# A one-core decoder block on Trainium2: DRAM writes of turned tiles on ScalarE's queue, residual additions three steps on, double units shifted by one, an FFN's initial chunks spread out

## The chip, the core and the metric

The kernel runs on one core of one Trainium2 chip. The core has a matrix engine (TensorE: PE for its matmuls and PEld for its weight loads in the profile), VectorE (DVE), ScalarE (ACT), GpSimd (POOL) and SyncE (SP). Each engine works through its own list of instructions in order and waits on semaphores where it needs another engine's result. DMAs are issued from SP, ACT or POOL. The metric is the time on the device in microseconds; lower is better.

## What is computed

One decoder block on 256 tokens of width 2048, all in float32. The reference, cut to its frame:

```python
h = x
h = h + 0.5 * swiglu(rms_norm(h, ffn1_norm), ffn1_w_gate, ffn1_w_up, ffn1_w_down)
n = rms_norm(h, mix_norm)
rq, rk, rv, rg, sq, sk, sv = split(n @ w_in)
ret = silu(rg) * group_norm(retention(rope(rq), rope(rk), rv)) * ret_gn_gain
swa = sliding_window_attention(rope(sq), rope(sk), sv, swa_sinks)
h = h + concat(ret, swa) @ w_out
h = h + memory_cross_attention(rms_norm(h, xa_norm), rms_norm(mem, mem_norm), xa_wq, xa_wkv, xa_wo)
h = h + 0.5 * swiglu(rms_norm(h, ffn2_norm), ffn2_w_gate, ffn2_w_up, ffn2_w_down)
out = rms_norm(h, final_norm)

def swiglu(x, w_gate, w_up, w_down):
    return (silu(x @ w_gate) * (x @ w_up)) @ w_down
```

The FFNs are 5632 wide and hold most of the weights. The memory has 256 tokens too.

## The kernel before

**Tiles and precision.** The residual h stands transposed in four tiles (blocks) of 128 partitions by 4 × 256. Weights come from HBM in pieces of 128 × 1024 floats (512 KB), on SP's queue, into eleven landing tiles `wf` (L65, L359). `split` (L368) makes of each piece a rounded part `wh` on ScalarE (L81) and a remainder `wl` on VectorE (L86); there are four tiles of each. A product is three matmuls (`three`, L638): high by high, high by low, low by high, all recorded as L641.

**Steps.** The whole block is one list of steps (`all_steps`, L322), run in order by `run_stream` (L386). A step uses one piece of weights in 12 matmuls of 512 columns. A `Unit` (L164) makes 512 output columns from the blocks of its input and calls `done` with two PSUM banks. Each step first issues the tasks that are due, then the splits of the step `LOOKAHEAD` = 3 places further on and the loads of 4 more; a plain step moves a counter, `clock`, by 1.

**Tasks.** `later(delay, fn)` (L113) puts off a piece of work to the step `delay` on. Its instructions on TensorE, ScalarE and VectorE are tied behind what those engines were given before (`run`, L143); instructions without such a tie can be moved by the compiler's scheduler. Up to step `FIRST` (L35, 15) all engines' orders are pinned as written, and the pieces of those steps are loaded ahead.

**Twins, chunks and double units.** In the FFNs a `Twin` (L185) makes gate and up (or two blocks of a down projection) together. One of the four input blocks is multiplied with seven products in place of eight, on sums and differences of quarters, as in Strassen's method. Such a product is a chunk, named P1 to P7, with 6 matmuls, one split and, for P4 to P7, a difference of two pieces on VectorE (L235); it moves `clock` by 0.5. P1, P5, P6 and P3 begin the four PSUM banks, P1, P5, P6 and P7 are followed by copies and additions (`keep` to `spread`, L260 to L275), and the plain steps of the other blocks add to the banks afterwards. A unit whose index is in `DOUBLE` (L39, used at L717) treats two blocks so and has 8 plain steps; another has 12. Every twin but the first of an FFN is `ahead`: its P1, P5, P6, P3, P7 are strewn among the steps of the unit before it. For the first twin of an FFN, P1 and P5 follow the last two steps of the gate and up of block 0, and P6, P3, P2, P7 come right after those. The sums of an input block, which the chunks multiply with, are made by `sums_of` (L297) in three tasks one step apart: scaling on ScalarE, four sums on VectorE (L290), the split.

**Turning a tile.** A result comes out with tokens on the partitions and is needed with features there. `cross` (L608) does this: two 32 × 32 block transposes on VectorE into `t4k` (L615), one step later a DMA write of 512 KB into a DRAM box (L619), another step later four DMA reads back in the other order (L624), and after `delay` steps a task that uses the tile. `TURN` is 6. There are two `t4k` tiles. Write and reads are issued by GpSimd.

**Residual additions.** `to_h` (L644) takes a projection's output through `cross` and adds it to h (L656) in the task at the end; that task also makes the next norm's scaled block (L81, L525) and its squares (L558, L562). `Norm.finish` (L567) adds the squares on VectorE (L570), sums them over the partitions with small matmuls (L573) and takes the root on GpSimd. The norm's scale is applied after the next projection, so matmuls can begin before the norm is finished.

The order of the work: FFN1 (blocks 0 to 3 of its width and a down projection of them, 4 to 7 and their down projection, 8 to 10 and theirs), the mixer's projections with retention and sliding-window attention between them, w_out, the projections and attention of the memory, xa_wo, FFN2 as FFN1, and the final norm.

Of the kernel before, what the change touches and what calls it, by code (L numbers as in the profile page):

```python
# [31 lines left out]
AHEAD = 4  # L32
TAIL = 4
WARM = 7
FIRST = 15  # L35
TURN = 6
SWA_EVERY = 5
LAND = 11
DOUBLE = (2, 4, 6, 8, 10)  # L39
P1, P5, P6, P3, P7, P2, P4 = range(7)  # L40


# [1 line left out]
def decoder_block(ctx: ExitStack, tc: tile.TileContext, a: dict, out: bass.AP):  # L44
    nc = tc.nc
# [276 lines left out]
    def all_steps():  # L322
        groups = []
        rest = list(units)
        while rest:
            u = rest.pop(0)
            x = u.steps()
            if u.then is not None:
                y = rest.pop(0).steps()
                nx, ny = (sum(z[1] == s[-1][1] for z in s) for s in (x, y))  # L330
                x = x[:-nx] + y[:-ny] + x[-nx:] + y[-ny:]
            groups.append((u, x))
        (u, x), (_, y) = groups[:2]
        x = [z for pair in zip(x, y) for z in pair]
        groups[:2] = [(u, x[:1] + [x[2], x[1]] + x[3:])]
        out = []
        for (u, x), (after, _) in zip(groups, groups[1:] + [(None, None)]):
            chunks = []
            if isinstance(u, Twin):
                if not u.ahead:  # L340
                    out += u.chunks((P6, P3, P2, P7))
                chunks = u.chunks((P2, P4) if u.ahead else (P4,))
            own, n = len(chunks), len(x)
            if isinstance(after, Twin) and after.ahead:
                chunks += after.chunks((P1, P5, P6, P3, P7))
            space = len(chunks) if len(chunks) > own else 2 * own
            for at, step in enumerate(x):
                out.append(step)
                if isinstance(after, Twin) and not after.ahead and at >= n - 2:
                    out += after.chunks((P1, P5)[at - n + 2 :][:1])  # L350
                for i, c in enumerate(chunks):
                    place = (2 * i + 1) * n // (2 * space)
                    if i < own:
                        place = min(place, n - 4)
                    if place == at:
                        out.append(c)
        return out
# [28 lines left out]
    def run_stream():  # L386
# [5 lines left out]
        for at in range(2, FIRST):  # L392
            if at % 4 == 0:
                load_x(at // 4, 0, 4)
            loaded[at] = load(steps[at][0].w, steps[at][3])
        ready = {}
        nxt = [0]

# [128 lines left out]
    class Norm:  # L527
# [4 lines left out]
        def __init__(self, gcol, name, delay, spread=False):  # L532
            self.gcol, self.delay, self.spreads = gcol, delay, spread
            self.blocks = {}
            self.rs = const.tile([P, 2], F32, tag=name, name=name)
            self.sums = self.rows = None
            self.left = 4
            self.ready = False

# [27 lines left out]
        def finish(self):  # L567

            x = self.sums
            nc.vector.tensor_tensor(x[:, :S], x[:, :S], x[:, S:], ALU.add)  # L570
            tp = tmp_ps()
            for t in range(2):
                nc.tensor.matmul(tp[:, t : t + 1], x[:, t * P : (t + 1) * P], ones, start=True, stop=True)  # L573
            ms = sm(2, "ms")
            nc.vector.tensor_scalar(ms, tp[:, :2], 1.0 / D, EPS, ALU.mult, ALU.add)
            nc.gpsimd.tensor_tensor(self.rs, ms, mhalf[:, :2], ALU.pow)
            self.ready = True
            if self.spreads:
                later(3, self.spread)
# [28 lines left out]
    def cross(src, then, delay=TURN):  # L608
# [7 lines left out]
        box = dram.tile([2 * P, 512], F32, tag="box", name=nm("box"))  # L616

        def write():
            nc.gpsimd.dma_start(box.rearrange("(t p) n -> p t n", t=2), z)  # L619

        def read():
            far = box.rearrange("(i r) (g n) -> g r i n", r=32, g=4)
            for g in range(4):
                nc.gpsimd.dma_start(z[32 * g : 32 * g + 32].rearrange("p t (i n) -> p (t i) n", i=4), far[g])  # L624
        later(1, write)
        later(2, read)
        later(delay, lambda: then([z[:, t, :].rearrange("p (i q j) -> p q i j", i=4, q=4) for t in range(2)]))

# [15 lines left out]
    def to_h(w, lhs, factor, blocks, norm=None, then=None, spare=0, seven=None, sums=None):  # L644

        def done(s, b):
# [6 lines left out]
            def add(out):  # L653
# [5 lines left out]
                    norm.stat([hT[b]])  # L659
                if then is not None:  # L660
                    then(b)
            cross(s, add, TURN + spare * (b < 3))
        for b in range(4):
            if seven is None:
                Unit(w, b, 512, lhs, lambda acc, b=b: done(acc, b), blocks, pair=True)
# [12 lines left out]
    def ffn(norm, w_gate, w_up, down, groups):  # L678
# [34 lines left out]
        for g, fbs in enumerate(groups):  # L713
            for b in fbs:
                done = functools.partial(both_done, b)
                if b > 0:
                    sevens = (2, 3) if b in DOUBLE else (3,)  # L717
                    plain = [x for x in range(4) if x not in sevens]
                    twin([w[2 * b : 2 * b + 2] for w in (w_gate, w_up)], norm.blocks, plain, sevens, sums, done)
                    continue  # L720
                for f, w in enumerate((w_gate, w_up)):
                    Unit(w, b, 512, norm.blocks, functools.partial(done, f), range(4), pair=True)
# [8 lines left out]
            later(4 * b - 1, lambda b=b: n1.block(b, [hT[b]]))  # L731
        later(4 * b + 2 * (b < 3), lambda b=b: n1.stat([hT[b]]))
    for b in (3, 2):
        later(22 - 4 * b, lambda b=b: sums_of(n1, b, input_sums[n1], 0))

    def load_x(b, lo, hi):
        nc.sync.dma_start(hT[b][:, lo:hi, :], a["x"][b * P : (b + 1) * P, lo:hi, :])
# [321 lines left out]
    def put_done(norm, dst, i, then=None):  # L1059

        def done(acc):
            s = [scaled(acc, t, 512, norm) for t in range(2)]

            def made(out):
# [4 lines left out]
                dst[i] = halves_of(out, x)  # L1069
                if then is not None:  # L1070
                    later(1, then)
            cross(s, made, TURN + 2)
        return done

    def v_done(i):
# [17 lines left out]
    def attend(i):  # L1093
# [30 lines left out]
        if i % 2 == 0:  # L1124
            st["p"] = p
        else:
            cross([st["p"], p], probs, TURN + 2)

    def values(i):
        v = vals[i]  # L1130
# [14 lines left out]
    for i in range(4):  # L1145
        Unit(a["xa_wv"], i, 512, nmem.blocks, v_done(i), range(4))

    n2 = Norm(G_FFN2, "n2", 5)
    to_h(a["xa_wo"], xo, 1.0, range(4), n2, lambda b: begin_ffn2(b))
    units[-3].then, units[-4].then = None, units[-3]  # L1150


# [69 lines left out]
    def begin_ffn2(b):  # L1222
        if b == 3:
            for b in (3, 2):
                later(31 - 10 * b, lambda b=b: sums_of(n2, b, input_sums[n2], 0))
            for b in range(4):
                later(19 + 12 * b, lambda b=b: turn_h(b))

# [85 lines left out]
```

## Time and profile before

| | us |
|---|---|
| median of 3 runs | 2171.98 (2167.69 to 2175.8) |
| the profiled execution | 2177.1 |
| its span, first to last instruction | 2175.3 |
| mean granted clock of TensorE | 0.994 |

The profile is of one execution. It names an instruction by engine, line and tiles: `DVE h L656` is VectorE's addition at line 656. Helpers record one line for all their uses: L81 is every copy on ScalarE, L86 every remainder on VectorE, L641 every matmul of a product. "Idle before" is the time an engine did nothing ahead of an instruction, with what ended it. Matmuls are pipelined, so the time between the starts of two tells more than the length of one. The granted clock (PEclk) is the share of TensorE's full clock. Sums over the span: DMAs moved 482.61 MB, of which 413.72 on SP's queue and 67.13 on GpSimd's.

### The profile page before, as it was taken

The page shows a single profiled execution, that of the slowest core. Times are in us where ns is not written, and L with a number is a line of the kernel's source. Part 1 is how long each engine was busy: PE and PEld are TensorE (multiplying, and loading weights), DVE is VectorE, ACT ScalarE, POOL GpSimd, SP SyncE. Part 2 cuts the span into 40 slices and gives each one's busy share as a digit, 9 for nine tenths or more (in the row PEclk, how much of TensorE's full clock was granted, in tenths as well). Part 3 has the DMA queues.
Part 4 walks back from the last instruction along what each step waited for, and adds up shares of the span by engine and source line. Part 5 has one row for each costly group of instructions (what it writes and reads, how often), then busy time and mean ns, then how long its engine had stood idle before and what let it go on. Part 6 is the DMA issues. An engine that isn't in the chain of part 4 may idle for free. (4 is left out here: it accounts for less than half of the span.)

```text
span 2175.3 us, 26666 instructions
## 1 busy us (share of the span) xinstructions
PE 2132.3 (98%) x9564; PEld 1758.9 (81%) x9564; DVE 1674.5 (77%) x1952; ACT 1212.3 (56%) x1517; POOL 208.0 (10%) x337
## 2 busy tenths in 40 slices
PE   9899999999999999999999999998999999999998
PEld 8788878888788877888788888886888878888886
DVE  7987889878875878787665555567898888888875
ACT  6655655656554654546455444455565556555654
POOL 0010110001001110101111110010111000000010
PEclk9999999999999999999999999999999999999999
DMA  8577776777778676767867875675787567776682
GB/s 301 171 239 238 221 240 216 242 223 246 236 240 251 219 210 209 209 221 234 243 199 242 246 228 174 195 236 149 217 284 244 194 213 225 225 220 200 203 283 88
DMA packets 213095, 482.61 MB, mean 222 GB/s; under 512 B 18145, under 2 KB 18145, under 8 KB 212961
## 3 DMA queue, kind: packets, MB, share of 16 engines
q1 hardware_dynamic: 191312, 413.72, 59.4%
q0 software_dynamic: 21504, 67.13, 11.4%
q8 instruction: 75, 1.23, 0.2%
q14 instruction: 60, 0.48, 0.1%
q10 hardware_dynamic: 144, 0.05, 0.0%
HBM read 445.17 MB, written 35.65 MB: 221 GB/s over the span
## 5 line engine op out<-in xcount | busy, mean ns | idle before, releaser
L81 ACT ACTIVATE wh<-wf 128x1024 fp32r<-128x1024 f32 (+1 forms) x891 | 929.0, 1053 | 803.6 <-PE acc L641 453.0
L86 DVE TENSOR_TENSOR wl<-wf,wh 128x1024 fp32r<-128x1024 f32 (+1 forms) x891 | 1068.7, 1215 | 395.6 <-ACT wh L81 382.9
L641 PE MATMUL acc<-wh,blk 128*128 128x512 f32 (+1 forms) x4336 | 1366.4, 389 | 2.0 <-ACT wh L81 2.0
L641 PEld LDWEIGHTS acc<-wh,blk 128*128 128x128 f32 x4336 | 815.6, 189 | 171.8 <-ACT wh L81 4.4
L641 PE MATMUL acc<-wl,blk 128*128 128x512 f32 (+1 forms) x2168 | 842.9, 389 | 3.8 <-DVE wl L86 3.8
L641 PE MATMUL tmp<-wh,blk 128*128 128x512 f32 x1736 | 567.6, 392 | 10.4 <-ACT wh L81 8.0
L641 PEld LDWEIGHTS acc<-wl,blk 128*128 128x128 f32 x2168 | 409.6, 189 | 87.1 <-DVE wl L86 5.7
L641 PEld LDWEIGHTS tmp<-wh,blk 128*128 128x128 f32 x1736 | 327.1, 189 | 83.4 <-ACT wh L81 12.5
L641 PE MATMUL tmp<-wl,blk 128*128 128x512 f32 x868 | 340.2, 392 | 8.9 <-DVE wl L86 8.9
L641 PEld LDWEIGHTS tmp<-wl,blk 128*128 128x128 f32 x868 | 163.9, 189 | 46.1 <-DVE wl L86 11.8
L235 DVE TENSOR_TENSOR wf<-wf,wf 128x1024 f32<-128x1024 f32 x152 | 182.8, 1220 | 13.5 <-DMA wf<-in_ffn_w_up 10.5
L619 POOL DMA_DIRECT2D box<-t4k x64 | 46.6, 728 | 1463.4 <-DVE t4k L615 1411.6
L624 POOL DMA_DIRECT2D t4k<-box x256 | 149.2, 589 | 282.8 <-DMA box<-t4k 196.8
L615 DVE STREAM_TRANSPOSE t4k<-t2k 128x512 f32<-128x512 f32 x96 | 64.7, 695 | 5.8 <-ACT t2k L81 5.7
L81 ACT ACTIVATE t2k<-acc 128x512 f32<-128x512 f32 x72 | 43.1, 598 | 26.3 <-PE acc L641 19.3
L86 DVE TENSOR_TENSOR blk<-t4k,blk 128x512 fp32r<-128x512 f32 (+2 forms) x72 | 44.2, 653 | 9.8 <-ACT blk L81 9.7
L81 ACT ACTIVATE t2k<-tmp 128x512 f32<-128x512 f32 x68 | 40.3, 593 | 20.4 <-PE tmp L641 13.1
L81 ACT ACTIVATE blk<-h,gains 128x256 fp32r<-128x256 f32 (+1 forms) x80 | 34.1, 496 | 18.1 <-DVE h L656 16.2
L81 ACT ACTIVATE blk<-t4k 128x512 fp32r<-128x512 f32 (+2 forms) x72 | 39.1, 595 | 7.1 <-DMA t4k<-box 7.1
L656 DVE TENSOR_TENSOR h<-h,t4k 128x512 f32<-128x512 f32 x40 | 25.8, 686 | 21.8 <-DMA t4k<-box 21.8
L525 DVE SCALAR_TENSOR_TENSOR blk<-h,gains,blk 128x256 fp32r<-128x256 f32 x64 | 26.7, 479 | 4.0 <-ACT blk L81 4.0
L253 DVE TENSOR_TENSOR tmp<-t2k,tmp 128x512 f32<-128x512 f32 x42 | 27.7, 689 | 0.3 <-ACT t2k L81 0.3
(137 smaller groups left out, 608.5 us busy)
## 6 DMA issues: line engine op xcount, KB each, us to landing
wf<-in_ffn_w_gate SPq DMA_DIRECT2D x176, 512.0 KB, 4.9
wf<-in_ffn_w_up SPq DMA_DIRECT2D x176, 512.0 KB, 5.2
wf<-in_ffn_w_down SPq DMA_DIRECT2D x176, 512.0 KB, 4.6
box<-t4k POOLq DMA_DIRECT2D x64, 512.0 KB, 3.9
t4k<-box POOLq DMA_DIRECT2D x256, 128.0 KB, 6.2
wf<-in_w_in_rqk SPq DMA_DIRECT2D x32, 512.0 KB, 4.7
wf<-in_w_in_rvg SPq DMA_DIRECT2D x32, 512.0 KB, 5.1
wf<-in_w_out SPq DMA_DIRECT2D x32, 512.0 KB, 5.3
```

Of the source, the lines that this page charges most:

```text
L81: return nc.scalar.activation(dst, src, AF.Copy, **kw)
L86: nc.vector.tensor_tensor(lo, src, hi, ALU.subtract)
L235: nc.vector.tensor_tensor(dst, p, q, ALU.subtract)
L253: nc.vector.tensor_tensor(out, a, b, ALU.add)
L525: nc.vector.scalar_tensor_tensor(x[:, k, 1, :], v[:, k, :], g, x[:, k, 0, :], ALU.mult, ALU.subtract)
L615: nc.vector.transpose(z[:, t, :].rearrange("p (g q j) -> p q g j", g=4, q=4), squares_of(v))
L619: nc.gpsimd.dma_start(box.rearrange("(t p) n -> p t n", t=2), z)
L624: nc.gpsimd.dma_start(z[32 * g : 32 * g + 32].rearrange("p t (i n) -> p (t i) n", i=4), far[g])
L641: nc.tensor.matmul(o, x, y, start=first, stop=last, skip_group_check=shared)
L656: nc.vector.tensor_tensor(v, v, out[t], ALU.add)
```

## The change

The DMA write of a turned tile is issued from ScalarE's queue, two steps after the transposes and not one; the reads stay with GpSimd in the same step as the write. Several delays change: the residual additions of the early down projections come three steps later for block 3 too, those of xa_wo two steps later for all blocks; keys, queries and probabilities are used one step earlier after their turn; the norm of FFN2 finishes 4 steps after its last squares and not 5; the sums of block 2 are made later in both FFNs. The double units are 3, 4, 6, 8 and 10. The chunks of an FFN's first twin are placed at P1 behind the fifth step from the end, P5 behind the third, P6 behind the second, P3 and P7 behind the last; P2 and P4 go among the twin's own steps. `FIRST` is 12 accordingly. The norm of an FFN then uses one of the twin's PSUM banks for its small matmuls.

```diff
-FIRST = 15
+FIRST = 12
-DOUBLE = (2, 4, 6, 8, 10)
+DOUBLE = (3, 4, 6, 8, 10)
...
             if isinstance(u, Twin):
-                if not u.ahead:
-                    out += u.chunks((P6, P3, P2, P7))
-                chunks = u.chunks((P2, P4) if u.ahead else (P4,))
+                chunks = u.chunks((P2, P4))
...
                 out.append(step)
-                if isinstance(after, Twin) and not after.ahead and at >= n - 2:
-                    out += after.chunks((P1, P5)[at - n + 2 :][:1])
+                if isinstance(after, Twin) and not after.ahead:
+                    out += after.chunks({n - 5: (P1,), n - 3: (P5,), n - 2: (P6,), n - 1: (P3, P7)}.get(at, ()))
...
             loaded[at] = load(steps[at][0].w, steps[at][3])
+        load_x(3, 0, 4)
...
             self.sums = self.rows = None
+            self.bank = tmp_ps
...
             nc.vector.tensor_tensor(x[:, :S], x[:, :S], x[:, S:], ALU.add)
-            tp = tmp_ps()
+            tp = self.bank()
...
         def write():
-            nc.gpsimd.dma_start(box.rearrange("(t p) n -> p t n", t=2), z)
+            nc.scalar.dma_start(box.rearrange("(t p) n -> p t n", t=2), z)
...
-        later(1, write)
+        later(2, write)
         later(2, read)
...
-            cross(s, add, TURN + spare * (b < 3))
+            cross(s, add, TURN + spare * (b < 3 or norm is not nmix))
...
                     twin([w[2 * b : 2 * b + 2] for w in (w_gate, w_up)], norm.blocks, plain, sevens, sums, done)
+                    if b == 1:
+                        norm.bank = functools.partial(twins[0].bank, 0, 1)
...
     for b in (3, 2):
-        later(22 - 4 * b, lambda b=b: sums_of(n1, b, input_sums[n1], 0))
+        later(46 - 12 * b, lambda b=b: sums_of(n1, b, input_sums[n1], 0))
...
-            cross(s, made, TURN + 2)
+            cross(s, made, TURN + 1)
...
-            cross([st["p"], p], probs, TURN + 2)
+            cross([st["p"], p], probs, TURN + 1)
...
-    n2 = Norm(G_FFN2, "n2", 5)
-    to_h(a["xa_wo"], xo, 1.0, range(4), n2, lambda b: begin_ffn2(b))
+    n2 = Norm(G_FFN2, "n2", 4)
+    to_h(a["xa_wo"], xo, 1.0, range(4), n2, lambda b: begin_ffn2(b), spare=2)
...
-                later(31 - 10 * b, lambda b=b: sums_of(n2, b, input_sums[n2], 0))
+                later(46 - 15 * b, lambda b=b: sums_of(n2, b, input_sums[n2], 0))
```

## The prediction

> **What bounds the kernel now.** I read the page's engine shares first, then a table of stretches of the span (busy time, instruction counts, granted TensorE clock), then the waits inside the bad stretches.
>
> ```profile
> span 2175.3 us, 26666 instructions
> ...
> PE 2132.3 (98%) x9564; PEld 1758.9 (81%) x9564; DVE 1674.5 (77%) x1952; ACT 1212.3 (56%) x1517; POOL 208.0 (10%) x337
> ```
>
> TensorE is busy for 98%, so a change that leaves its matmuls alone, as this one does, can only win stalls. The table (columns: us, busy us and count for each engine, granted clock, DMA share, GB/s) shows where they are.
>
> ```profile
> core 0: us, PE busy (x) PEld busy (x) DVE busy (x) ACT busy (x) POOL busy (x), PEclk, DMA share, GB/s
> 100.00:300.00 200.00, 200.00 (x884) 165.62 (x883) 169.04 (x169) 119.79 (x133) 21.37 (x35) 1.00 0.77 241
> 44.00:75.00 31.00, 23.73 (x92) 17.85 (x92) 28.01 (x33) 16.58 (x23) 4.85 (x6) 0.89 0.52 161
> 300.00:335.00 35.00, 32.16 (x132) 25.32 (x131) 28.79 (x31) 17.39 (x21) 3.05 (x5) 0.95 0.69 200
> 555.00:595.00 40.00, 37.06 (x158) 28.90 (x157) 34.20 (x36) 20.90 (x24) 3.05 (x5) 1.00 0.72 216
> ...
> 1050.00:1070.00 20.00, 17.35 (x72) 13.95 (x71) 12.22 (x15) 7.17 (x8) 3.76 (x6) 0.91 0.72 230
> 1260.00:1275.00 15.00, 13.85 (x73) 11.63 (x72) 10.26 (x17) 7.74 (x15) 2.48 (x4) 1.00 0.70 227
> 1450.00:1500.00 50.00, 44.69 (x182) 35.63 (x181) 32.27 (x42) 24.01 (x33) 4.70 (x6) 0.93 0.59 185
> 1500.00:1530.00 30.00, 25.08 (x98) 19.02 (x97) 25.85 (x30) 18.12 (x24) 3.08 (x5) 0.94 0.60 171
> ```
>
> The first row is saturation: 200 / 884 = 0.226 us for a matmul, so 2.72 us for a step of 12 and 1.36 us for a chunk of 6. Length less count times 0.226 is what a stretch loses: 10.2 us in 44–75 (start of the first FFN), 5.1 in 300–335, 4.3 in 555–595, 3.7 in 1050–1070, 16.7 in 1450–1530 (start of the second FFN). In 1260–1275, with other shapes, the idle time is 1.2. Together 41 us. Part of a loss is the clock: 0.95 over 35 us costs 1.7 us, 0.93 over 50 us 3.5, 0.89 over 31 us 3.4.
>
> Waits, each as total, times, longest. VectorE's in 285–310, 536–566, 1030–1060 and 1400–1480; then TensorE's in 300–335, 555–595 and 1050–1075:
>
> ```profile
> DVE h L656 <- DMA t4k<-box: 4.9, 1, 4.9
> DVE h L656 <- DMA t4k<-box: 4.0, 1, 4.0
> DVE h L656 <- DMA t4k<-box: 4.7, 1, 4.7
> DVE h L656 <- DMA t4k<-box: 8.2, 2, 5.4
> PE tmp L641 <- DVE wl L86: 2.6, 1, 2.6
> PE tmp L641 <- DVE wl L86: 2.0, 2, 1.7
> PE tmp L573 <- DVE t2k L570: 2.7, 1, 2.7
> ```
>
> L656 is the residual addition; it waits for the turned tile and all of VectorE's splits wait behind it. 4.9, 4.0 and 4.7 us of VectorE became 2.6, 1.7 and 2.7 us of TensorE: about 2.2 us are absorbed, the rest arrives.
>
> **The change, part by part.** TensorE's sum is unchanged: the number of double units is still five, and each chunk is issued once.
>
> *DRAM writes to ScalarE's queue, issued two steps after the transposes and not one.* POOL's instructions in 275–300, then of pairs after w_out and in the cross-attention (start, us, what, idle before and releaser):
>
> ```profile
> 278.57 0.72 POOL L619 DMA_DIRECT2D box<-t4k  x1 [28.24 <-DVE t4k L615]
> 284.16 2.33 POOL L624 DMA_DIRECT2D t4k<-box  x4 [4.86 <-issue]
> 287.34 0.72 POOL L619 DMA_DIRECT2D box<-t4k  x1 [0.86 <-DVE t4k L615]
> 295.32 2.41 POOL L624 DMA_DIRECT2D t4k<-box  x4 [7.26 <-DMA box<-t4k]
> ...
> 1034.00 0.72 POOL L619 DMA_DIRECT2D box<-t4k  x1
> 1042.57 2.33 POOL L624 DMA_DIRECT2D t4k<-box  x4 [7.85 <-ACT wh L81]
> ...
> 1244.21 0.72 POOL L619 DMA_DIRECT2D box<-t4k  x1 [1.85 <-DVE t4k L615]
> 1253.74 2.33 POOL L624 DMA_DIRECT2D t4k<-box  x4 [8.81 <-DMA box<-t4k]
> ```
>
> The reads at 284.16 started 5.6 us after their write, those at 295.32 8.0 us after theirs, which was queued behind the four reads of the tile before. So were the writes at 1034.00 and 1244.21: 8.6 and 9.5 us. A write in another queue isn't: some 3 us sooner for the second of a pair. Against that stands the later issue. Two rows of ScalarE's queue, the group of the transposes, two rows of DMA landing (median us) and one of the engines' waits on this tile:
>
> ```profile
> 1443.99 1.06 ACT L81 ACTIVATE wh<-wf 128x1024 fp32r<-128x1024 f32 x1 [1.66 <-PE acc L641]
> ...
> 0.74 0.40 ACTq L94 DMA_DIRECT2D gains<-in_gains  x1
> ...
> L615 DVE STREAM_TRANSPOSE t4k<-t2k 128x512 f32<-128x512 f32 x96 | 64.7, 695 | 5.8 <-ACT t2k L81 5.7
> ...
> box<-t4k POOLq DMA_DIRECT2D x64, 512.0 KB, 3.9
> ...
> out<-t2k SPq DMA_DIRECT2D x8, 256.0 KB, 2.7
> ...
> DMA t4k<-box: 33.7, 13
> ```
>
> ScalarE goes in step with TensorE, each split freed by TensorE (first row). A write placed two steps on sits behind the split that waits for the end of the first step: 2.7 + 1.1 = 3.8 us after the unit ends, where POOL issued at about 1.6 (two transposes of 0.7, third row, and the hand-over). So 2.2 us later. The landing from ScalarE's queue isn't in the trace; between 2.7 (half the bytes, SP) and twice that, 5.4, I take 3.9, as now. What queues behind the issue is ScalarE's splits: 64 issues of 0.4 us are 26 us on an engine that is 56% busy and whose idle time is mostly waits on TensorE, so nothing while the transposes are done when it gets there; without that cover the 26 us would show. The last row is the engines' total wait for turned tiles, 33.7 us in 13 waits: 21.8 are the five of L656, 11.9 us in eight waits remain. Those come 2.2 us later, about what is absorbed; I charge **3 us** in all, bounds 0 and 18 (8 × 2.2).
>
> [...] No run here yet shows a write on ScalarE's queue.
>
> *Residual additions three steps on.* Block 3 of the early down projections adds 8.2 us later than now; its tile was 4.9 and 4.0 us late. Gain 2.6 + 1.7 of clock at 300–335, 1.7 + 0.3 at 555–595: **6.3 us**. What remains there (0.8 and 2.3) is VectorE's load at the next chunks, untouched. The additions of w_out keep their delay, but the late one (4.7 us, pair at 1034.00) was the second of a pair, and its 2.7 us of TensorE stand before 1060: **3.0** of 3.7 with the clock's share. TURN + 1 for keys, queries and probabilities gives a step back; the late probabilities (1244.21) were the second of a pair too: **1.0** of 1.2.
>
> *First FFN.* Before, P1 and P5 stand behind the last two steps and P6, P3, P2, P7 follow at once; now P1 stands four steps before the end, P5 two, P6 one, P3 and P7 behind the last step, P2 and P4 among the next unit's steps.
>
> ```profile
> L86 DVE TENSOR_TENSOR wl<-wf,wh 128x1024 fp32r<-128x1024 f32 (+1 forms) x891 | 1068.7, 1215 | 395.6 <-ACT wh L81 382.9
> ...
> L235 DVE TENSOR_TENSOR wf<-wf,wf 128x1024 f32<-128x1024 f32 x152 | 182.8, 1220 | 13.5 <-DMA wf<-in_ffn_w_up 10.5
> ...
> 44.57 1.22 DVE L86 TENSOR_TENSOR blk<-blk,blk 128x1024 fp32r<-128x1024 f32 x1
> ...
> 51.86 0.39 PE L641 MATMUL tmp<-wh,blk 128*128 128x512 f32 x1
> ```
>
> P1, P5, P6, P3, P7 cost VectorE five splits and three differences, 8 × 1.2 = 9.7 us, against 5 × 1.36 = 6.8 of TensorE; an ordinary step costs 1.2 against 2.72. Five chunks in five steps make 15.8 against 20.4: they fit, where six behind two steps, 13.2 against 13.6 before norm, gate and up, didn't. Moving the double unit takes five chunks out of the next unit, and block 2's sums (4 × 0.42 + 1.2 = 2.9 us) go eight steps on. What is late next: P1 needs the sums of block 3, ready at 45.8 (third row). It starts at 51.9 now (fourth row), three steps earlier is 43.7: a new wait of 2.1 us. With 1 us for other jostling 3.2 of 10.2 stay: **7.0** gained, bounds 0 and 10.2. The fewer initial loads only change where SP's orders are written, not their sequence, and the norm borrows a bank that only P6, later, fills: nothing for either, hidden by the steps between; without them a wait like the 2.1.
>
> *Second FFN.* VectorE's rows in 1466–1490:
>
> ```profile
> 1472.21 1.23 DVE L235 TENSOR_TENSOR wf<-wf,wf 128x1024 f32<-128x1024 f32 x1 [5.62 <-DMA wf<-in_ffn_w_up]
> ...
> 1474.49 1.29 DVE L656 TENSOR_TENSOR h<-h,t4k 128x512 f32<-128x512 f32 x2
> ...
> 1485.97 1.23 DVE L86 TENSOR_TENSOR blk<-blk,blk 128x1024 fp32r<-128x1024 f32 x1
> ...
> 1488.25 0.41 DVE L570 TENSOR_TENSOR t2k<-t2k 128x256 f32<-128x256 f32 x1
> ```
>
> All its additions come two steps later, which removes the 8.2 us of L656 waits. From the addition to the sums VectorE took 12.7 us, to the norm's sum 14.2. Now (norm's delay 4 and not 5, P1 three steps sooner) four steps, 10.9 us, lie between the addition and both; block 2's sums again go later. So TensorE waits some 3 us there, long enough for the clock to drop (3.4 as in 44–75). 6.4 of 16.7 stay: **10.2** gained, bounds 0 and 16.7.
>
> Sum: 6.3 + 3.0 + 1.0 + 7.0 + 10.2 − 3 = 24.5. The profiled execution took 2177.1, 1.8 over its span; it would take 2152.6. The median of the runs shown, 2171.98, lies 5.1 lower: **2147.5**.
>
> **The rivals.**
> *A: VectorE is the bound at both starts.* 28.01 of 31 and 25.85 of 30 us busy speak for it, 32.27 of 50 against: P1 meets unfinished sums and the 17.2 vanish into new waits. 2171.98 − 7.3 = 2164.7.
> *B, slower: the write stands in ScalarE's order.* If the transposes are late (VectorE behind) ScalarE stops, its splits with it, and the tile is a further step late. Price: the eight waits left and the five residual additions that keep their delay (w_out's four, the first FFN's last), 13, each 2.7 + 2.2 − 2.2 = 2.7 us of TensorE, and 1.7 for the clock: 57 us less the 27.5 gained, 2202. It decides from a write 5 us or more after the unit's end. Against: POOL's writes above were released by the transposes (DVE t4k), which take 1.4 us of the 3.8.
> *C: the second write of a pair still waits for the reads before it,* because they share the engines and not only the queue: pairs stay 8.0 us apart, the 3.0 and 1.0 are lost, 2151.5. For it: 295.32 shows the time and not its reason; against it: the lone write, beside the same weight loads, took 5.6. [...]
> *D: everything goes,* the waits at P1 being filled with the next steps' matmuls: 2172 − 41 = 2131.
>
> **How the numbers follow.** Forecast 0.50, A 0.18, B 0.08, C 0.14, D 0.10. The range 2131–2170 runs from D to A with its crossings charged 5 us more; it leaves out B and the edges. Half a per cent (10.9 us, about what a measurement of this kernel can tell from no change) is passed below 2161.1: forecast, C and D, and a little of A: faster 0.76. The rest of A is the same, 0.16. Slower is B, 0.08.
>
> **What would show it.** Right: POOL only reads; the second of a pair starts its reads within 6 us of its write; L656 no longer waits; the stretch 300–335 has clock 1.00; 44–75 and 1450–1530 hold some 30 more matmuls each. Wrong: ScalarE idle before its writes, waits of TensorE on `blk` L86 or L570 over 4 us, or as many matmuls in the two starts as now.

## The result and the profile after

| | before | after |
|---|---|---|
| median of 4 runs, us | 2171.22 (2167.69 to 2175.8) | 2149.19 (2140.03 to 2151.0) |
| ratio, with its 95% interval | | 0.9889 (0.9855 to 0.9923) |
| the profiled execution, us | 2177.1 | 2140.03 |
| mean granted clock | 0.994 | 0.998 |

The changed kernel is 1.1% faster by the ratio, and its median lies 1.7 us from the forecast of 2147.5. Its other three runs took 2148.18 to 2151.0, so the first profile is of an unusually short execution. I profiled the same kernel again (the run `x1_changed_again`: that execution 2148.38, median 2148.45) and read the changed kernel mostly there. The head of that page:

```profile
span 2146.6 us, 26717 instructions
...
PE 2121.2 (99%) x9564; PEld 1751.1 (82%) x9564; DVE 1674.2 (78%) x1952; ACT 1209.6 (56%) x1517; POOL 161.2 (8%) x273
```

The matmuls are as many as before, VectorE's and ScalarE's busy time is the same. The span is 28.7 us shorter: 17.6 us of that is idle time of TensorE (43.0 before, 25.4 now), and 11.1 us is its busy time (2132.3 before), because the same matmuls ran at a reduced clock for less of it. The traces' clock records, without the end of the span, hold 23.9 us at half clock before and 3.4 in x1. So over a third of the gain is the clock's. POOL's 64 fewer instructions are the writes. The second profile's table of stretches, with the columns of the table of before; the rows answer in turn to 44–75, 300–335, 555–595, 1050–1070, 1260–1275 and the two of 1450–1530:

```profile
44.00:75.00 31.00, 29.56 (x130) 23.47 (x130) 27.51 (x31) 17.57 (x24) 4.09 (x5) 1.00 0.63 187
285.00:320.00 35.00, 34.67 (x153) 28.38 (x152) 32.24 (x35) 18.82 (x21) 2.30 (x4) 1.00 0.78 237
540.00:580.00 40.00, 37.66 (x164) 30.29 (x163) 36.31 (x38) 21.95 (x25) 2.31 (x4) 1.00 0.75 235
1035.00:1055.00 20.00, 17.98 (x75) 14.49 (x74) 11.94 (x15) 7.18 (x8) 3.96 (x5) 0.91 0.81 254
1240.00:1255.00 15.00, 14.83 (x77) 12.56 (x76) 10.02 (x17) 8.69 (x17) 0.00 (x0) 1.00 0.78 221
1434.00:1484.00 50.00, 50.00 (x223) 41.15 (x222) 39.07 (x49) 32.00 (x43) 3.92 (x5) 1.00 0.61 185
1484.00:1514.00 30.00, 30.00 (x134) 24.86 (x133) 26.90 (x33) 19.29 (x24) 2.33 (x4) 1.00 0.77 242
```

The number to read is the count behind PE. The start of the first FFN holds 130 matmuls where it held 92, the start of the second 357 where it held 280: TensorE hardly stops there (1.4 us idle in 44–75, none at the second FFN), and the clock is 1.00. VectorE does about as much in 44–75 (27.51 us against 28.01) and more at the second FFN (65.97 against 58.12), so it wasn't the bound that rival A took it for; its work only lies where TensorE doesn't wait for it. One row is about as bad as before: in 1035–1055, behind w_out, there are 75 matmuls at a clock of 0.91.

The table below puts all kernels of this study side by side. It is worked out from the traces and is no view of the profile: the time between the starts of two matmuls, less 0.2267 us for each 512 columns, is what was lost there; it is added up over stretches cut at the same amount of matmul work in every kernel. Each row is one execution, and an execution can lie some us off its kernel's median: x3's is its fastest run, 5.1 us below the median, and u1's its slowest, 1.9 above.

```
us lost (profiled execution)    FFN1  behind    next  behind  memory    FFN2   after   rest     sum
                               start   early   chunks  w_out  attent.  start    it
                                      downs
before                          11.1     9.1     1.0     5.4     2.1    18.1     0.0    27.6    74.4
after, first profile             5.1     2.6     1.6     1.1     0.7     0.6     1.1    24.5    37.3
x1 changed kernel again          4.4     3.2     2.3     4.9     1.1     0.6     1.6    27.3    45.6
c1 changed kernel again          5.7     2.1     1.6     3.2     0.9     0.6     1.8    28.1    43.9
x2 write by GpSimd               4.9     2.5     2.3     2.0     0.7     0.6     7.2    26.6    46.8
x3 additions back                5.1     8.9     2.2     2.0     0.7     7.3     4.5    26.2    56.8
u1 early downs' additions back   5.2    12.6     1.2     3.0     0.7     0.6     5.8    29.3    58.4
x4 chunks back                   6.6     1.6     2.4     1.0     0.7     4.5     0.9    29.0    46.7
y4 doubles back                  9.7     1.7     1.8     2.8     2.1     2.4     0.0    24.0    44.4
y2 before + additions           12.2     1.7     1.0     2.3     6.2     6.1     0.0    26.2    55.7
y6 before + doubles              6.3     7.4     1.9     2.3     1.0    13.6     1.4    27.0    61.0
w2 two more doubles shifted      5.8     1.0     3.0     3.7     0.7     0.6     1.9    32.0    48.5
z2 w_out's additions later       5.7     1.3     2.9     1.0     1.9     0.6     4.9    28.1    46.4
z3 z2 and doubles back           8.7     2.3     2.6     1.0     0.7     2.4     0.0    26.7    44.4
```

Before to x1: 6.7 us came from the start of the first FFN, 5.9 from behind the early down projections, 17.5 from the start of the second FFN, 0.5 from behind w_out, 1.0 from the memory's attention; nearly 3 us were lost elsewhere. The columns "next chunks" (some 300 to 360 us of matmul work from the first matmul, right behind the first early down projection) and "after it" (some 1465 to 1525) lost 1.0 and 0.0 before.

### The profile page after: what moved, and what is told of

Its sections match the earlier page's. It is cut to its first block, busy times and chain, and to the rows that moved or that the text cites. A ratio compares the mean times of both kernels' runs of the same rounds, so it can differ in the third digit from the quotient of the medians.

```text
span 2138.3 us, 26717 instructions
## 1 busy us (share of the span) xinstructions
PE 2118.2 (99%) x9564; PEld 1750.4 (82%) x9564; DVE 1674.6 (78%) x1952; ACT 1210.7 (57%) x1517; POOL 160.2 (7%) x273
## 4 chain that ended last, share of the span: by engine, by line
PE 90%; DVE 5%; DMA 2%; issue 1%; ACT 1%; POOL 0%; ACTq 0%; SPq 0%; POOLq 0%; DVEq 0%
PE acc L641 63%; PE tmp L641 25%; DVE wl L86 3%; DMA t4k<-box 1%; ACT wh L81 1%; DVE wf L235 1%; DMA wf<-in_ffn_w_gate 0%; DMA wf<-in_ffn_w_up 0%; PE tmp L875 0%; DVE tmp L253 0%; DVE t4k L615 0%; DVE t2k L692 0%; DVE blk L86 0%; PE tmp L856 0%; DVE acc L253 0%
## 5 line engine op out<-in xcount | busy, mean ns | idle before, releaser
L641 PE MATMUL tmp<-wh,blk 128*128 128x512 f32 x1728 | 561.3, 390 | 4.1 <-ACT wh L81 4.1
L235 DVE TENSOR_TENSOR wf<-wf,wf 128x1024 f32<-128x1024 f32 x152 | 182.9, 1221 | 16.7 <-DMA wf<-in_ffn_w_up 12.8
L615 DVE STREAM_TRANSPOSE t4k<-t2k 128x512 f32<-128x512 f32 x96 | 64.4, 695 | 5.1 <-ACT t2k L81 4.9
L656 DVE TENSOR_TENSOR h<-h,t4k 128x512 f32<-128x512 f32 x40 | 25.7, 684 | 5.7 <-DMA t4k<-box 5.7
L524 DVE SCALAR_TENSOR_TENSOR blk<-h,gains,blk 128x256 fp32r<-128x256 f32 x64 | 26.7, 480 | 4.2 <-ACT blk L81 4.2
L253 DVE TENSOR_TENSOR acc<-t2k,acc 128x512 f32<-128x512 f32 x42 | 27.7, 692 | 0.0
```

Of the source, the lines that this page charges most:

```text
L235: nc.vector.tensor_tensor(dst, p, q, ALU.subtract)
L253: nc.vector.tensor_tensor(out, a, b, ALU.add)
L524: nc.vector.scalar_tensor_tensor(x[:, k, 1, :], v[:, k, :], g, x[:, k, 0, :], ALU.mult, ALU.subtract)
L615: nc.vector.transpose(z[:, t, :].rearrange("p (g q j) -> p q g j", g=4, q=4), squares_of(v))
L641: nc.tensor.matmul(o, x, y, start=first, stop=last, skip_group_check=shared)
L656: nc.vector.tensor_tensor(v, v, out[t], ALU.add)
```

## The experiments

The theory after the result: the residual additions and the starts of the FFNs brought the gain, the queue of the write brought little. The rival: the write on its own queue brought the early tiles, and the additions need it.

### What each part is worth in the changed kernel

**The changed kernel again.**

> The changed kernel once more, for a second profile. Its profiled execution took 2140.0 us and its other runs 2148 to 2151, at the same granted clock. Theory: the starts of both FFNs and the early down projections lose as little as in the first profile (5.1 us and under 1 us at the FFN starts), and the missing 8 to 11 us lie in waits that end with a DMA, scattered over the span. Rival: the waits at the FFN starts come back in a usual execution, 5 us or more there.

Measured: 2148.45, ratio 0.9886 (0.987 to 0.9902). The ratio is confirmed; the profile is the one read above. Where the first profile had 91 matmuls behind w_out in 1035–1055 this one has 75, so that stop is there in some executions and not in others.

**The write back on GpSimd, one step after the transposes.**

```diff
-            nc.scalar.dma_start(box.rearrange("(t p) n -> p t n", t=2), z)
+            nc.gpsimd.dma_start(box.rearrange("(t p) n -> p t n", t=2), z)
-        later(2, write)
+        later(1, write)
```

> The changed kernel with the DRAM write back on GpSimd's queue, one step after the transposes. Theory (the delays and the placement of the chunks do it, the queue does not): within 5 us of the changed kernel, no wait of the residual additions. Rival (the queue does it, because the second of a pair no longer stands behind the reads): 7 us or more slower, with waits on w_out's second block (4.7 us of VectorE, 2.7 of TensorE and the clock's 1.7) and on the probabilities (1.1).

Measured: 2148.76, ratio 0.9884 (0.9865 to 0.9903), the same as x1 on the same chip. The move of the write, its queue and its step together, is worth nothing that these runs can tell; queue and step weren't taken apart. Why, in rows: first the landing of the write in x1 and in x2 (KB, median us from issue to landing), then the pair of tiles behind w_out in each (start, us, what, idle before and releaser); of x1 first ScalarE's, then POOL's.

```profile
box<-t4k ACTq DMA_DIRECT2D x64, 512.0 KB, 5.2
```

```profile
box<-t4k POOLq DMA_DIRECT2D x64, 512.0 KB, 4.2
```

```profile
1013.51 0.37 ACTq L619 DMA_DIRECT2D box<-t4k  x1
...
1019.03 0.37 ACTq L619 DMA_DIRECT2D box<-t4k  x1
```

```profile
1019.68 2.30 POOL L624 DMA_DIRECT2D t4k<-box  x4 [39.13 <-DVE wl L86]
1026.56 2.30 POOL L624 DMA_DIRECT2D t4k<-box  x4 [4.58 <-ACT wh L81]
```

```profile
1012.71 0.72 POOL L619 DMA_DIRECT2D box<-t4k  x1 [30.39 <-DVE t4k L615]
1017.44 2.33 POOL L624 DMA_DIRECT2D t4k<-box  x4 [4.01 <-DMA box<-t4k]
1019.76 0.72 POOL L619 DMA_DIRECT2D box<-t4k  x1
1028.07 2.32 POOL L624 DMA_DIRECT2D t4k<-box  x4 [7.59 <-ACT wh L81]
```

On GpSimd the first of the pair takes 4.7 us from write to reads and the second 8.3; on ScalarE 6.2 and 7.5. The second is 0.8 us quicker from its write, the first 1.4 slower. By the clock the second starts its reads 1.5 us earlier (1026.56 against 1028.07) and the first 2.2 later. What this pair's second tile wins, the first loses, and so do most lone tiles: over the 42 tiles that are in no pair the median from write to reads is 5.3 us in x1 and 4.3 in x2 (worked out from the two traces). The median landing from ScalarE's queue took a microsecond more (5.2 us against 4.2).

**The additions back** to their delays of before, with the norm's delay of 5.

```diff
-            cross(s, add, TURN + spare * (b < 3 or norm is not nmix))
+            cross(s, add, TURN + spare * (b < 3))
-    n2 = Norm(G_FFN2, "n2", 4)
-    to_h(a["xa_wo"], xo, 1.0, range(4), n2, lambda b: begin_ffn2(b), spare=2)
+    n2 = Norm(G_FFN2, "n2", 5)
+    to_h(a["xa_wo"], xo, 1.0, range(4), n2, lambda b: begin_ffn2(b))
```

> The changed kernel with the old delays of the residual additions (block 3 of the early down projections, xa_wo, FFN2's norm). Theory: slower by 15 us: 4.3 and 2.3 at the two early down projections, where the tile lands some 21 us after its unit and the addition comes after 16, and 8 or more at FFN2's start. Rival (the queue alone frees the additions): within 4 us.

Measured: 2164.66, ratio 0.9955 (0.9939 to 0.997): 16.2 us slower than x1. The stretches of x3 that answer to the second and sixth row of x1:

```profile
285.00:320.00 35.00, 31.46 (x137) 25.23 (x136) 27.84 (x29) 18.36 (x21) 2.30 (x4) 1.00 0.74 232
...
1437.00:1487.00 50.00, 46.29 (x196) 37.33 (x196) 34.59 (x45) 25.54 (x36) 3.94 (x5) 0.97 0.61 187
```

Sixteen matmuls fewer behind the early down projection, 27 fewer at the second FFN: the stops of before are back, in the old places. Most of the gain is the additions'. The edit takes back three things at once: block 3 of the early down projections, xa_wo's blocks and the norm's delay. Only the first of them is taken back alone, in u1 below.

**The chunks back** to where they stood before.

```diff
-FIRST = 12
+FIRST = 15
...
-                chunks = u.chunks((P2, P4))
+                if not u.ahead:
+                    out += u.chunks((P6, P3, P2, P7))
+                chunks = u.chunks((P2, P4) if u.ahead else (P4,))
...
-                if isinstance(after, Twin) and not after.ahead:
-                    out += after.chunks({n - 5: (P1,), n - 3: (P5,), n - 2: (P6,), n - 1: (P3, P7)}.get(at, ()))
+                if isinstance(after, Twin) and not after.ahead and at >= n - 2:
+                    out += after.chunks((P1, P5)[at - n + 2 :][:1])
...
-        load_x(3, 0, 4)
```

> The changed kernel with the first twin's chunks where they were (P1 and P5 behind the last two steps, P6, P3, P2, P7 at once behind them, 15 initial steps); double units and sums stay shifted. Theory: slower by 12 to 16 us, 8 at FFN1's start and 5 to 8 at FFN2's, with waits on wl L86 while VectorE is busy for over 90%. Rival (shifting the double unit and the sums was enough): within 4 us.

Measured: 2150.01, ratio 0.9891 (0.9875 to 0.9907). Not the 12 to 16 us slower that I expected but 1.6, within what the runs scatter. In the table the two starts lose 2.2 and 3.9 us more than in x1, and behind w_out 3.9 less. My theory that the spreading alone makes the two starts falls, so the next question was what does.

### Each part alone, on the kernel before and on the changed one

**The additions alone**, on the kernel before (the diff is the reverse of x3's; the write stays with GpSimd).

> The kernel before with the later residual additions alone (block 3 of the early down projections, xa_wo, FFN2's norm delay). Theory: this is the larger part by itself, 14 to 17 us faster than before, about as much as undoing it cost (16.2): no clock drop and no wait of L656 at the early down projections and at FFN2's norm. Rival (the parts need each other, since late additions meet chunks in one heap): under 8 us faster.

Measured: 2154.8, ratio 0.991 (0.9894 to 0.9927), 20.5 us faster than the kernel before on that chip, more than the 14 to 17 expected. So the additions don't need the write on its own queue. In the table of losses that is 7.4 us behind the early down projections and 12.0 at the second FFN; the first FFN's start stays at 12.2, and the memory's attention loses 4.1 more in this execution.

**The doubles back** in the changed kernel, chunks spread.

```diff
-DOUBLE = (3, 4, 6, 8, 10)
+DOUBLE = (2, 4, 6, 8, 10)
...
-        later(46 - 12 * b, lambda b=b: sums_of(n1, b, input_sums[n1], 0))
+        later(22 - 4 * b, lambda b=b: sums_of(n1, b, input_sums[n1], 0))
...
-                later(46 - 15 * b, lambda b=b: sums_of(n2, b, input_sums[n2], 0))
+                later(31 - 10 * b, lambda b=b: sums_of(n2, b, input_sums[n2], 0))
```

> The changed kernel with the double units back at 2, 4, 6, 8, 10 and block 2's sums at their old steps; the chunks stay spread. Theory (shifting the double unit lightens VectorE at an FFN's start, spreading the chunks is a second way to the same, so one is enough): at most 4 us slower than the changed kernel. Rival (the shift is the part that counts): 8 us or more slower, with waits on wl L86 in 55 to 75.

Measured: 2146.98, ratio 0.9874 (0.9858 to 0.989). Taking the shift out doesn't make the kernel slower.

**The doubles alone**, on the kernel before (the diff is the reverse).

> The kernel before with the shift of the double unit and of block 2's sums alone. Theory: 5 to 9 us faster than before, most of it in 44 to 75 (10.2 us lost before), less at FFN2's start, which still has the late addition in front. Rival (the shift alone is worth nothing without the spread chunks): within 2 us of before.

Measured: 2163.55, ratio 0.9953 (0.9935 to 0.9971), 11.8 us faster, more than the 5 to 9 expected. So the shift is worth something while the chunks stand in a heap. Stretch 44–75 of y2 (neither), y4 (chunks spread), y6 and x4 (doubles shifted), in this order, each from its own table:

```profile
44.00:75.00 31.00, 23.77 (x88) 17.72 (x87) 27.09 (x32) 15.44 (x22) 4.83 (x6) 0.83 0.53 166
```

```profile
44.00:75.00 31.00, 25.15 (x103) 18.78 (x102) 29.48 (x35) 17.89 (x23) 0.71 (x1) 0.98 0.51 164
```

```profile
44.00:75.00 31.00, 27.08 (x116) 20.75 (x115) 28.59 (x32) 17.21 (x22) 4.84 (x6) 1.00 0.54 154
```

```profile
44.00:75.00 31.00, 27.06 (x116) 20.72 (x115) 28.66 (x31) 17.17 (x22) 4.09 (x5) 1.00 0.57 160
```

At this place both help, and in these single executions they add: 88 or 92 matmuls with neither, 103 with the chunks spread, 116 with the doubles shifted, 130 with both. Over the kernel they don't: with the additions made later, neither gives 0.991 (y2, its write on GpSimd), the chunks alone 0.9874, the doubles alone 0.9891, both 0.9886 to 0.9894. Some of what the shift wins it returns a little later, where the double unit now stands. 100–120 in x1 and in y4:

```profile
100.00:120.00 20.00, 18.94 (x83) 14.96 (x82) 18.09 (x19) 8.96 (x11) 2.30 (x4) 1.00 0.69 226
```

```profile
100.00:120.00 20.00, 20.00 (x90) 16.57 (x89) 16.05 (x18) 12.75 (x14) 0.00 (x0) 1.00 0.79 241
```

With the doubles shifted 83 matmuls fit (76 and 80 in the other two profiles of the changed kernel) where 90 do without, and VectorE is busier. Behind the second FFN's start it is the same: "after it" has 0.9 to 7.2 us in the kernels with the doubles shifted and 0.0 in those without. These returns don't account for all: the first is already in the first column, and there x1 still stands 5.3 us better than y4. "Rest" can't settle it, since it has 24.0 and 26.7 without the shift (y4, z3) and 24.5 to 28.1 in the three profiles of the changed kernel. Why the shift gains nothing over the whole kernel stays open.

**Two more doubles shifted**, 5 for 4 and 9 for 8, since stops were left behind the early down projections where a double unit's sums and differences fall.

```diff
-DOUBLE = (3, 4, 6, 8, 10)
+DOUBLE = (3, 5, 6, 9, 10)
```

> A step on from the changed kernel: double units 3, 5, 6, 9, 10, so that the first unit behind each early down projection is a single one too. Theory (a double first unit loads VectorE with ten chunks in twelve steps, here 2 to 3 us lost at 317, 570, 1745 and 1998): 5 to 9 us faster than the changed kernel. Rival (the load only moves a unit on): within 3 us.

Measured: 2150.71, ratio 0.9895 (0.9876 to 0.9915). A miss: behind the early down projections only 1.0 us is lost, but "rest" has 32.0 where c1 has 28.1, and the chunks after the first of them 3.0 where it has 1.6. That VectorE's load is still there, only elsewhere, is what these sums suggest; it wasn't traced wait by wait.

### How much hangs on one block, and the stop behind w_out

**The changed kernel beside these** (no edit), as their measure.

> The changed kernel again, as the measure for the next three on the same chip: 2147 to 2151 us, its FFN starts as before (4.4 and 2.1 us lost), the wait of the memory's norm near 1043 between 0 and 4 us from one profile to the next.

Measured: 2148.6, ratio 0.9894 (0.9879 to 0.991).

**Block 3 of the early down projections alone** back to six steps; xa_wo keeps its later additions.

```diff
-            cross(s, add, TURN + spare * (b < 3 or norm is not nmix))
+            cross(s, add, TURN + spare * (b < 3 or norm not in (None, nmix)))
```

> The changed kernel with only the early down projections' block 3 added after 6 steps again; xa_wo's additions stay late. Theory: slower than the changed kernel by the two waits there, 3.6 to 4.3 and 2.0 to 2.7 us with the clock's share, so 5 to 7 us, and the rest of the 16 belongs to xa_wo. Rival (the waits there overlap with VectorE's load at the next chunks, which stays): 2 us or less.

Measured: 2159.28, ratio 0.994 (0.9927 to 0.9952): 10.7 us slower than c1, more than expected. One block of two projections costs this much (12.6 − 2.1 = 10.5 in the table of losses; the two profiled executions lie 14.4 us apart, 4.0 of it in "after it"). Waits of VectorE in 285–310 and of TensorE there (total, times, longest), then the two stretches:

```profile
DVE h L656 <- DMA t4k<-box: 6.6, 1, 6.6
```

```profile
PE tmp L641 <- DVE wl L86: 4.3, 1, 4.3
```

```profile
285.00:320.00 35.00, 30.71 (x129) 24.91 (x128) 26.79 (x28) 17.76 (x20) 2.31 (x4) 0.95 0.74 220
540.00:580.00 40.00, 36.66 (x156) 29.94 (x155) 32.71 (x34) 19.45 (x22) 3.71 (x7) 0.96 0.72 223
```

With the write on ScalarE's queue and two steps on, the first addition waits 6.6 us where it waited 4.9 before, and TensorE 4.3 where it waited 2.6; the second addition waits 5.7 where it waited 4.0. But x3 has the same code here, and its two additions, in 280–312 and in 530–570, wait less:

```profile
DVE h L656 <- DMA t4k<-box: 5.6, 1, 5.6
DVE h L656 <- DMA t4k<-box: 4.0, 1, 4.0
```

So the later write costs an addition between nothing and 1.7 us, by the execution. x3 loses 8.9 us behind the early down projections and u1 12.6, and nearly all of the difference is the clock: 1.00 in both stretches of x3, 0.95 and 0.96 in u1, which is 3.4 us over 35 and 40. In the changed kernel the additions don't wait here at all, so that the later addition hides whatever the later write costs. The two edits are not independent.

**w_out's additions two steps later**, in the changed kernel.

```diff
-    to_h(a["w_out"], mixT, 1.0, (2, 3, 0, 1), None, out_done)
+    to_h(a["w_out"], mixT, 1.0, (2, 3, 0, 1), None, out_done, spare=2)
```

> A step on: the changed kernel with w_out's additions two steps later as well. Theory (L656 still waits 4.0 us in two waits there, and the memory's norm pays for it with up to 4 us of TensorE): no wait of L656 in 1000 to 1060 and 1 to 4 us faster than the changed kernel. Rival (the norm's lateness has another cause, VectorE's load): the same time, with TensorE still waiting on L570 there.

Measured: 2148.15, ratio 0.989 (0.9875 to 0.9905), equal to c1. The waits of VectorE in 1000–1062, in x1 and then in z2:

```profile
DVE h L656 <- DMA t4k<-box: 4.0, 2, 2.1
```

```profile
DVE wl L86 <- ACT wh L81: 17.7, 14, 2.0
DVE ms L575 <- PE tmp L573: 0.7, 1, 0.7
```

The addition's wait is gone, and less is lost behind w_out (1.0 us; 3.2 in c1, 4.9 in x1). That the one brings the other isn't shown: the first profile of the changed kernel, with the same 4.0 us of waits of L656, lost 1.1 there. The time isn't shorter: "after it" has 4.9 where c1 has 1.8. In z2's trace TensorE waits there once, and VectorE ahead of it:

```profile
PE acc L641 <- DVE wl L86: 2.9, 1, 2.9
```

```profile
DVE wf L235 <- DMA wf<-in_ffn_w_up: 2.4, 1, 2.4
```

A difference of two pieces of weights (L235) waits for a load, with VectorE's splits behind it. x2 (7.2), u1 (5.8) and x3 (4.5), kernels with other edits, have a loss at that place too. Whether z2's gain is lost by its own edit or by the way the loads fell in that execution isn't settled.

**Both: doubles back and w_out later**, the version that the table of losses suggests.

> The same with the double units at 2, 4, 6, 8, 10 and block 2's sums at their old steps, which was not slower in the last comparison (2147.0). Theory: equal to the run with w_out's additions later within 3 us, about 2145; FFN1's start loses some 5 us more and the units behind the down projections some 3 us less. Rival (the double units' place matters once the rest is out of the way): 5 us or more apart.

Measured: 2145.41, ratio 0.988 (0.9867 to 0.9893), the lowest median of the study and 3.2 us below c1 on the same chip. The intervals overlap; that it beats the changed kernel isn't shown.

The move of the write alone, on the kernel before, wasn't tried; only its undoing was (x2). The earlier use of keys, queries and probabilities, the twin's bank for the norm and the smaller `FIRST` outside of x4 weren't taken back by themselves.

## Why the prediction was right, step by step

**Residual additions: right.** The forecast took 6.3 us from behind the early down projections. x1 shows 9.1 − 3.2 = 5.9, the first profile 6.5, c1 7.0. Undoing it costs 10.7 (u1), more than doing it gained: in u1's profile the clock drops at both places (0.95 and 0.96), where it dropped at one before (0.95 and 1.00), and each addition waits 1.7 us longer. The charge for a later write, 2.2 us a tile, was too high for these additions, which show 0 to 1.7 (x3, u1), and it falls only where no delay covers it; the change had added that delay.

**Write's queue: wrong.** "A write in another queue isn't: some 3 us sooner for the second of a pair" came out as 1.5 us by the clock behind w_out, with the first 2.2 later. Over the eleven tiles whose write followed another's within 10 us before, the mean from write to reads is 8.0 us before, 7.6 in x1 and 7.5 in x2 (worked out from the traces): 0.4 us sooner, and no less with the write on GpSimd. The gains that were put down to it came all the same, in part: w_out's 3.0 us as 0.5 (x1), 2.2 (c1) and 4.3 (first profile), the probabilities' 1.0 as 1.0, 1.2 and 1.4. x2 has 3.4 and 1.4 with the write on GpSimd, so the queue isn't what brings them; what does isn't shown. The landing, taken at 3.9 between 2.7 and 5.4, was 5.2. Nor was the −3 for later writes found: with the write early on GpSimd (x2) the time is the same. Where the waits for turned tiles went is seen in the waits of ScalarE and VectorE on them, before and in x1:

```profile
DVE h L656 <- DMA t4k<-box: 21.8, 5, 5.4
ACT blk L81 <- DMA t4k<-box: 9.2, 6, 3.0
```

```profile
ACT blk L81 <- DMA t4k<-box: 25.8, 16, 4.2
DVE h L656 <- DMA t4k<-box: 6.7, 3, 2.7
```

VectorE waits 15.1 us less, ScalarE 16.6 us more. The sum didn't fall. x2 has 9.0 on VectorE and 16.0 on ScalarE, so VectorE's relief comes mostly from the later additions and some 10 us on ScalarE from the later write. The sign that L656 no longer waits failed: 6.7 us are left, 4.0 of them behind w_out. But 21.8 us on VectorE, which TensorE waits for at the next split, cost a good part of what they last; 25.8 us in 16 pieces on ScalarE, 56% busy, cost little that can be seen. Rival C was right that the second of a pair still waits: behind w_out it takes 7.5 us from its write to its reads, and not the 6 that the forecast named as its sign. As for C's reason, x1's DMA table counts the packets of SP's, GpSimd's and ScalarE's queues at 60.9, 7.2 and 4.3% of the time of the core's 16 DMA engines; that the second write waits because the queues share them isn't shown. C's price, the loss of the 3.0 and the 1.0, didn't follow from the wait. Rival B's 13 stops of ScalarE for late transposes didn't come either: in x1's table of waits one wait of ScalarE, of 1.5 us, ends with a transpose of L615. By x1 against x2 the other issuer saved time of issuing, 0.37 us for an issue in place of 0.72, and the kernel's time is the same (2148.45 and 2148.76).

**First FFN: right in kind, with one cost that isn't there and one return that wasn't foreseen.** Forecast 7.0, measured 38 matmuls × 0.226 = 8.6 in the stretch, of which 100–120 gives 1.2 back (20 − 83 × 0.226). By the table, which counts both, the gain is 6.7 in x1, 6.0 in the first profile and 5.4 in c1. The step that failed is "P1 needs the sums of block 3". It doesn't: P1's left operand in the table of products is a pair of quarters, (0, 0), and is taken from the block itself; only P5, P6, P7 and P3 take sums. x1's TensorE and VectorE there:

```profile
40.42 0.39 PE L641 MATMUL tmp<-wh,blk 128*128 128x512 f32 x1
```

```profile
39.88 1.55 DVE L290 TENSOR_TENSOR blk<-blk 128x256 f32<-128x256 f32 x4
...
44.82 1.22 DVE L86 TENSOR_TENSOR blk<-blk,blk 128x1024 fp32r<-128x1024 f32 x1
```

P1 starts at 40.42 while the sums are being added, and runs 4.4 us ahead of their split. The new wait of 2.1 us was charged to a dependence that isn't there.

**Second FFN: right in kind, too small by the same step and by VectorE's time.** Forecast 10.2 of 16.7, measured 17.5 of 18.1. The first profile of the changed kernel, TensorE and then VectorE:

```profile
1464.61 0.61 PE L573 MATMUL tmp<-ones,t2k 128*128 128x1 f32 x4
1465.08 0.48 PE L641 MATMUL tmp<-wh,blk 128*128 128x512 f32 x1
...
1471.32 0.39 PE L641 MATMUL tmp<-wh,blk 128*128 128x512 f32 x1
```

```profile
1452.61 1.29 DVE L656 TENSOR_TENSOR h<-h,t4k 128x512 f32<-128x512 f32 x2
...
1464.13 0.42 DVE L570 TENSOR_TENSOR t2k<-t2k 128x256 f32<-128x256 f32 x1
1464.47 1.22 DVE L86 TENSOR_TENSOR blk<-blk,blk 128x1024 fp32r<-128x1024 f32 x1
```

The norm's small matmuls meet a sum that is ready, P1 follows them while the sums' split still runs (to 1465.7), and P5, the first to need it, comes at 1471.32. No wait of 3 us and no drop of the clock (1.00 in 1429–1479); the 6.4 us that the forecast left there were 0.6. From the addition to the norm's sum VectorE takes 11.9 us (1452.61 to 1464.55), not the 14.2 of before.

**What the forecast didn't have:** the shift of the doubles and the spreading of the chunks lighten VectorE in the same steps, either without the other gives the time of both within the scatter (y4, x4), and the shift returns part of its gain later. The forecast took both as one edit with one answer.

**Why the total fits all the same.** In the five places named by the forecast x1 gained 31.6 us, against 27.5 forecast before the charge; elsewhere nearly 3 were lost (rival D's 41 didn't all go), which stands in for the −3 by chance: x2, without the later writes, loses more there (7.2 us after the second FFN's start alone). That is 28.8 by the table against 24.5. The profiled execution of before, though, lay 5.9 us over the median of its four runs, and by the medians the gain is 22.0 (here), 25.2 (x1) and 24.0 (c1). The underestimates and the choice to subtract a constant 5.1 us from both sides cancelled.

## What to carry to other kernels

Look at what is queued behind a waiting instruction before looking at what it waits for: setting the use of a transfer two or three steps on took 20.5 us off this kernel (y2), and moving the write to another queue nothing that could be told (x2). Before a new wait is charged to a dependence, read the operand in the code that makes the instruction; P1 used no sums, and two terms hung on it. A stop of TensorE can cost more than it lasts, since the clock dropped behind some of them (to 0.50 for 3.4 us behind one of 2.0 in x1): count time at a reduced clock beside idle time. Two edits that lighten the same engine at the same place must be measured alone and together: at that place they added, over the kernel they did not.

## What the hardware showed unexpectedly

**The same 512 KB landed later from ScalarE's queue**: median 5.2 us against 4.2 from GpSimd's with the same weight loads running (3.9 to 4.2 in before, x2, y2 and y6, 5.1 to 5.4 in the three profiles of the changed kernel, x3 and u1), though the issue itself took half as long (0.37 us against 0.72). The write is also a step later there, so that queue and moment aren't taken apart.

**The clock fell after a short stop and not after a longer one.** Behind w_out in x1, then behind the early down projection in x3, waits of TensorE; then x1's stretch right behind the first:

```profile
PE tmp L573 <- DVE t2k L570: 2.0, 1, 2.0
```

```profile
PE tmp L641 <- DVE wl L86: 3.5, 2, 3.2
```

```profile
1046.10:1049.50 3.40, 3.40 (x9) 2.71 (x10) 1.31 (x2) 0.00 (x0) 2.81 (x4) 0.50 0.84 270
```

After 2.0 us the granted clock was 0.50 for 3.4 us, which makes the 0.91 of 1035–1055 (1.7 us lost); after 3.2 us it stayed 1.00 in 285–320. In w2 it fell to 0.50 at 1784 behind two waits of 1.3 and 0.9 us. In the trace of before, five stops of 2.4 to 3.0 us were each followed, within 3 us, by a clock of 0.50, three times for 3.4 us and twice for 6.8. What decides whether a stop is followed by one isn't shown. So the 1.7 us for the clock that the forecast counted behind the early down projection is a chance and not a price: there the clock was 0.95 in the kernel before and in u1, and 1.00 in x3.

**Executions of one kernel differ, perhaps by where weight loads fall.** The changed kernel's three profiles span 2138.3, 2146.6 and 2144.9 us. Of the 8.3 us between the first two, 3.8 are the stop behind w_out; the rest is spread over many places. VectorE's differences of weights (L235) wait longer for their loads in the second profile than in the first, and 14.0 us in the third:

```profile
DVE wf L235 <- DMA wf<-in_ffn_w_up: 12.8, 10, 3.1
```

```profile
DVE wf L235 <- DMA wf<-in_ffn_w_up: 16.8, 11, 3.0
```

That the loads cause the rest is read from these waits and was not tested.
